# Hybrid streaming encoder layer on one core: a bias table stored from 128 partitions, VectorE in GpSimd's place in the projections, and two steps moved at the start of the windowed attention

## The chip, the cores and the metric

The kernel runs on one core of a Trainium2 chip. The metric is the device time of one execution in microseconds; the time of a kernel is the median of its runs. One execution is also recorded by the hardware profiler, and all durations inside the kernel come from that one.

## The reference

One layer is applied to a prompt of 1024 tokens and to a sample of 64 tokens that continues an older sequence; the width is 1024. Everything is float32.

```
rq, rk, rv, rg, sq, sk, sv, ga, gb = split(rms_norm(x) @ w_in)
A = retention(rope(rq), rope(rk)/16, rv)          # 4 heads of 256, blocks with decay
A = (rms_norm(A) * silu(rg)) @ w_ret_out
s = sq @ sk.T / 8 + bias                          # 16 heads of 64, own chunk of 64 and 128 keys before
B = softmax(s with a learned sink per head) @ sv @ w_swa_out
x += (sigmoid(ga) * A + sigmoid(gb) * B) @ w_mix_out
x += cross_attention(rms_norm(x), memory keys and values)   # 4 heads, 256 memory tokens
x += swiglu(rms_norm(x))
y = rms_norm(x)
```

`bias` is a T5 table of 32 buckets by 16 heads, looked up by the distance of query and key. Retention also returns its last state, the attention its last keys and values, and the memory its keys and values.

## The kernel before

Tokens lie along the free dimension, 1088 of them (1024 and 64), cut into two halves of 544. Each float32 operand of a large product is split into a high part (a cast to fp32r on ScalarE, L124) and a low part (source minus high part on VectorE, L125, in `split`), and a product is three matmuls on TensorE: high by high, high by low, low by high (L223, L224, L226 in `multiply`; L157 to L159 in `mm3`). Large products use Strassen's scheme (`strassen`): seven products of sums of weight blocks. `weight_ops` forms those sums in the raw weight tile, on the engine `sums_by`: VectorE (L191 to L197) until the last query projection, GpSimd (L201 to L207) from there on.

The projections come first (`project_phase`). For each of four retention heads the loop projects keys, queries, and values, the last two lines of each `rotated` step being the sum and difference of the rotary embedding (L649, L650); from the second head on it projects a pair of attention query tiles as well, whose result is multiplied by the token's inverse norm `rstd` (L619 in `project`). Results pass through `stage` tiles to HBM scratch (`d_qkv`, `d_sq`, `d_skv`, `d_gate`). After each head's projections stands `retention(h)`: per block of 256 tokens it loads `ks`, `vf` and `qs` back from `d_qkv`, transposes them on TensorE (`pk`, L768), forms scores (`pss`), the state (`pkv`) and the output (`po`). `ret_out` then normalises the output: ScalarE squares (L890), a row of small VectorE steps (L893, `rsqrt_steps` L320 to L325, L329), ScalarE scales (L896), TensorE turns it back (`pb`, L902). The next head's projections lie between these steps, to keep TensorE occupied.

Between the second and third head stands `bias_table`: a one-hot matmul (L573) looks up the 16 heads' 256 distances, VectorE scales them into `rb` (L574), and one DMA writes `d_rb`, where each head's row of 256 stands 64 times, so that a later load with a stride of 255 reads it shifted per query. The sinks follow (L580 to L585).

`begin_swa` and `swa` are the windowed attention: per half chunk, scores on TensorE (`pss`, L1006, one PSUM tile), add of the bias with minimum and maximum on VectorE (`nm`, L1016), exponentials on ScalarE (L1022, L1024), sum and reciprocal on VectorE (L1025, L1026), scaling on GpSimd (L1028). Pieces of other work fill TensorE between them (`filler`): first the last head of the memory values, `pd` scaled by `mtok` into `swin` (L1202), then the product with `w_ret_out`, whose operands `ret` are loaded and cast by `first_loads` (high parts) and finished by `first_low` (ten low parts, L1155). Those pieces have two PSUM tiles.

The order on each engine is set by a scheduler that models the program's time; `issue_after(x)` holds an instruction behind x in that order. `self.marks` has, for each scores step issued so far, the VectorE instruction that ends its maxima (L1020) and its last exponential; `first_low` is called when two steps have been issued. SyncE's queue (SP) issues most DMAs, in order.

Of the kernel before, what the change touches and what calls it, by code (L numbers as in the profile page):

```python
# [11 lines left out]
F32 = mybir.dt.float32  # L12
F32R = mybir.dt.float32r
AF = mybir.ActivationFunctionType
ALU = mybir.AluOpType
# [4 lines left out]
P = 128  # L20
# [7 lines left out]
BLK = 256  # L28
# [81 lines left out]
class Kernel:  # L110
# [453 lines left out]
    def bias_table(self):  # L564

        nc, io = self.nc, self.io
        t = self.ra.tile([P, BLK + 16], F32, tag="sf", bufs=1, name="table")
        rb = self.ra.tile([P, 2, BLK], F32, tag="o", bufs=1, name="rb")[:16]
        table, onehot = t[:32, BLK:], t[:32, :BLK]
        self.load(table, io["rel_bias"])  # L570
        self.load(onehot, io["c_onehot"])
        pb = self.norm_psum("pb")
        nc.tensor.matmul(pb[:16, :256], table, onehot, start=True, stop=True)  # L573
        nc.vector.tensor_scalar(rb, pb[:16, :256].unsqueeze(1).broadcast_to([16, 2, 256]), 8.0, None, ALU.mult)  # L574
        self.store(self.d_rb.rearrange("h (i c) -> h i c", c=512),
                   rb.rearrange("p a b -> p (a b)").unsqueeze(1).broadcast_to([16, 32, 512]))
        row = self.np.tile([P, 16], F32, tag="row", bufs=1, name="row")[:1]
        self.load(row, io["sinks"])
        ps = self.norm_psum("ps")
        nc.tensor.matmul(ps[:, :16], self.ones[:1, :], row, start=True, stop=True)  # L580
        for e in range(2):
            rows = slice(e * 64, (e + 1) * 64)
            nc.vector.tensor_copy(self.sinks[rows, :], ps[rows, :16].rearrange("p (a b) -> p a b", b=2)[:, :, e])
        self.minus = self.np.tile([P, 16], F32, tag="row", bufs=1, name="minus")[:, :NPAIR]
        nc.vector.tensor_scalar(self.minus, self.sinks, -1.0, None, ALU.mult)  # L585

    def project_phase(self):
        nc, tc, io = self.nc, self.tc, self.io
        with ExitStack() as ctx:
# [11 lines left out]
            half = lambda t: slice(t * HALF, (t + 1) * HALF)  # L601
            flat = lambda o: o.rearrange("p b c -> p (b c)")

            def staged():
                count[0] += 1
                return stage[(count[0] - 1) % len(stage)]

            def taken(ps, sb):
                o = staged()
                if sb is None:  # L610
                    self.last_copy = nc.scalar.copy(o, ps).ins
                else:
                    nc.vector.tensor_tensor(out=o, in0=ps, in1=sb, op=ALU.add)  # L613
                return flat(o)

            def project(w, put, act=None, other=None):
                def emit(i, t, ps, sb):
                    o = taken(ps, sb)
                    (nc.vector if act is not None else nc.gpsimd).tensor_tensor(  # L619
                        out=o, in0=o, in1=self.rstd[:, half(t)], op=ALU.mult)  # L620
                    if act is not None:
                        nc.scalar.activation(o, o, act)
                    if other is not None:
                        r = op.tile([P, HALF], F32, tag="other", bufs=4, name="other")
                        self.load(r, other(i)[:, half(t)])
                        nc.gpsimd.tensor_tensor(out=o, in0=o, in1=r, op=ALU.mult)
                    put(i, t, o)
                cast = self.last_cast
                self.strassen(w, self.ops, emit)
                return cast  # L630

            def rotated(w, h, j, before=None):

                done = {}

                def emit(i, t, ps, sb):
                    done[i, t] = taken(ps, sb)
                    if (1 - i, t) not in done:
                        return
                    a, b = done[0, t], done[1, t]  # L640
                    cos, sin = (rope[:, i, half(t)] for i in range(2))
                    sa, sb = flat(staged()), flat(staged())
                    tt = nc.vector.tensor_tensor
                    tt(out=sa, in0=a, in1=sin, op=ALU.mult)
                    tt(out=sb, in0=b, in1=sin, op=ALU.mult)
                    tt(out=a, in0=a, in1=cos, op=ALU.mult)
                    tt(out=b, in0=b, in1=cos, op=ALU.mult)
                    tt = tt if h < 2 else nc.gpsimd.tensor_tensor
                    tt(out=a, in0=a, in1=sb, op=ALU.subtract)  # L649
                    tt(out=b, in0=b, in1=sa, op=ALU.add)  # L650
                    self.store(self.d_qkv[j, 2 * h, :, half(t)], a)
                    self.store(self.d_qkv[j, 2 * h + 1, :, half(t)], b)
                self.strassen(w, self.ops, emit, before=before)
# [67 lines left out]
            for idx, w, act in ((1, "w_ga", AF.Sigmoid), (0, "w_rg", AF.Silu), (2, "w_gb", AF.Sigmoid)):  # L721
                for m in range(0, KT, 2):
                    if (idx, m) == (1, 6):
# [4 lines left out]
                        op = ctx.enter_context(tc.tile_pool(name="op", bufs=1, reuse_waits="tile"))  # L728
# [399 lines left out]
    def ld(self):  # L1128
        self.lds.append(self.lds.pop(0))
        return self.lds[-1]  # L1130
# [19 lines left out]

    def first_low(self):

        with self.tc.issue_after(self.marks[-1][0]):
            for a, hi, lo in self.first:
                self.nc.vector.tensor_tensor(out=lo, in0=a, in1=hi.bitcast(F32), op=ALU.subtract)  # L1155

# [29 lines left out]
    def filler(self):  # L1186

        nc, tc, io = self.nc, self.tc, self.io
        if True:
            ld, rets = self.ld, self.rets  # L1190
            self.first_low()
            us, h = self.first_units, H - 1
            for t in range(2):
                ps = self.dense_psum()
                for k in range(KT):
                    x = self.ms[k][:, :, t * P:(t + 1) * P]
                    self.mm3(ps[:, :256], x[:, 0], x[:, 1], *us[k // 4][k % 4], k == 0, k == KT - 1)
                    if k == 3:
                        yield
                o = ld()[:, :256]  # L1200
                with tc.high_priority():
                    self.values_out = nc.scalar.mul(o, ps[:, :256], self.mtok[:, t:t + 1]).ins  # L1202
                nc.gpsimd.dma_start(self.d_mv[h, :, t, :], o)
                nc.gpsimd.dma_start(io["o_mv"][t * P:(t + 1) * P, h * 256:(h + 1) * 256], o)
                yield
# [8 lines left out]
            for m, c in order:  # L1214
# [9 lines left out]
                for ps in self.pieces(u, rets, c0, n):  # L1224
                    if step in extra:
                        i, j = extra.pop(step)
# [666 lines left out]
```

## Time and profile before

| | |
|---|---|
| median of 3 runs | 2172.07 us (2171.89 to 2172.37) |
| profiled execution | 2170.14 us, of which the span of its instructions is 2168.3 us |
| mean granted TensorE clock | 0.996 |
| TensorE matmul busy | 2134.6 us (98%) |
| VectorE busy | 1547.7 us (71%) |
| ScalarE busy | 875.0 us (40%) |
| GpSimd busy | 588.8 us (27%) |
| DMA | 290.84 MB, mean 134 GB/s |

In the rows that follow PE is TensorE's matmul, PEld its weight load, DVE VectorE, ACT ScalarE, POOL GpSimd and SP SyncE; a q behind the name is the engine's queue. Times are from the span's start. A row of the groups gives line, engine, operation, tiles, shape and count, then busy time and the mean ns of one, then the idle time in front. A row of the waits gives who waited for whom, then microseconds in total, times, and the longest. A row of the windows gives a stretch, its length, the busy time of PE, PEld, DVE, ACT and POOL with the count of instructions, the granted TensorE clock, the share of the DMA engines and GB/s.

### The profile page before, as it was taken

The page shows a single profiled execution, that of the slowest core. Times are in us where ns is not written, and L with a number is a line of the kernel's source. Part 1 is how long each engine was busy: PE and PEld are TensorE (multiplying, and loading weights), DVE is VectorE, ACT ScalarE, POOL GpSimd, SP SyncE. Part 2 cuts the span into 40 slices and gives each one's busy share as a digit, 9 for nine tenths or more (in the row PEclk, how much of TensorE's full clock was granted, in tenths as well). Part 3 has the DMA queues.
Part 4 walks back from the last instruction along what each step waited for, and adds up shares of the span by engine and source line. Part 5 has one row for each costly group of instructions (what it writes and reads, how often), then busy time and mean ns, then how long its engine had stood idle before and what let it go on. Part 6 is the DMA issues. An engine that isn't in the chain of part 4 may idle for free. (4 is left out here: it accounts for less than half of the span.)

```text
span 2168.3 us, 41740 instructions
## 1 busy us (share of the span) xinstructions
PE 2134.6 (98%) x16371; PEld 2082.8 (96%) x16371; DVE 1547.7 (71%) x2874; ACT 875.0 (40%) x1896; POOL 588.8 (27%) x484
## 2 busy tenths in 40 slices
PE   9999999999999999999999999999999999999997
PEld 9999999999999997889999999999999999999997
DVE  8986978776677558656545565778777777877597
ACT  8333434353434357543233333333322222344243
POOL 0001211233253124540000000015556555523531
PEclk9999999999999999999999999999999999999998
DMA  7334453444345476336442121522342333384333
GB/s 268 118 128 120 135 140 104 138 126 154 120 142 178 154 228 218 119 108 209 133 147 96 40 69 46 161 67 91 126 149 89 105 117 100 117 311 151 112 116 112
DMA packets 169894, 290.84 MB, mean 134 GB/s; under 512 B 39298, under 2 KB 96546, under 8 KB 169698
## 3 DMA queue, kind: packets, MB, share of 16 engines
q1 hardware_dynamic: 161666, 269.00, 38.8%
q0 software_dynamic: 3424, 10.82, 1.4%
q10 hardware_dynamic: 4608, 8.36, 1.0%
q8 instruction: 129, 2.11, 0.4%
q14 instruction: 67, 0.55, 0.1%
HBM read 196.95 MB, written 91.16 MB: 133 GB/s over the span
## 5 line engine op out<-in xcount | busy, mean ns | idle before, releaser
L125 DVE TENSOR_TENSOR wq<-raw,wq 128x512 fp32r<-128x512 f32 (+1 forms) x499 | 435.4, 877 | 131.8 <-ACT wq L124 128.2
L124 ACT CAST wq<-raw 128x512 fp32r<-128x512 f32 (+1 forms) x499 | 301.8, 614 | 539.8 <-PE pq L226 210.5
L224 PE MATMUL pq<-T,wq 128*128 128x272 f32 x1832 | 492.2, 289 | 0.1
L223 PE MATMUL pq<-T,wq 128*128 128x272 f32 x1832 | 490.7, 288 | 1.3 <-DVE stage L613 0.6
L224 PE MATMUL pq<-B,wq 128*128 128x272 f32 x1592 | 427.0, 288 | 0.1
L223 PE MATMUL pq<-B,wq 128*128 128x272 f32 x1592 | 425.7, 288 | 0.0
L226 PE MATMUL pq<-T,wq 128*128 128x272 f32 x1832 | 382.9, 289 | 1.9 <-DVE wq L125 1.9
L223 PEld LDWEIGHTS pq<-T,wq 128*128 128x128 f32 x1832 | 344.4, 188 | 2.1 <-ACT xsq L499 0.8
L224 PEld LDWEIGHTS pq<-T,wq 128*128 128x128 f32 x1832 | 344.2, 188 | 1.2 <-issue 0.8
L226 PE MATMUL pq<-B,wq 128*128 128x272 f32 x1592 | 331.7, 289 | 0.0
L224 PEld LDWEIGHTS pq<-B,wq 128*128 128x128 f32 x1592 | 299.1, 188 | 0.8 <-issue 0.4
L223 PEld LDWEIGHTS pq<-B,wq 128*128 128x128 f32 x1592 | 299.0, 188 | 0.1
L226 PEld LDWEIGHTS pq<-T,wq 128*128 128x128 f32 x1832 | 289.8, 189 | 3.9 <-DVE wq L125 2.4
L201 POOL TENSOR_TENSOR raw<-raw 128x512 f32<-128x512 f32 (+1 forms) x44 | 62.2, 1413 | 802.4 <-DVE rs_r L322 455.6
L226 PEld LDWEIGHTS pq<-B,wq 128*128 128x128 f32 x1592 | 251.7, 189 | 0.9 <-issue 0.7
L274 DVE TENSOR_TENSOR u<-pq,u 128x544 f32<-128x544 f32 x177 | 127.2, 719 | 84.8 <-PE pq L226 84.6
L619 POOL TENSOR_TENSOR stage<-stage,rstd 128x544 f32<-128x544 f32 x20 | 31.6, 1584 | 323.0 <-ACT rstd L514 203.7
L613 DVE TENSOR_TENSOR stage<-pq,u 128x544 f32<-128x544 f32 x112 | 80.3, 718 | 31.6 <-PE pq L226 27.8
L157 PE MATMUL pd<-xc,wq 128*128 128x256 f32 (+1 forms) x256 | 74.5, 291 | 0.0
L1541 POOL TENSOR_TENSOR stage<-stage,rstd_f 128x544 f32<-128x544 f32 x40 | 63.9, 1607 | 39.1 <-ACT stage L1540 39.1
L159 PE MATMUL pd<-xc,wq 128*128 128x256 f32 (+1 forms) x256 | 74.1, 290 | 0.0
L158 PE MATMUL pd<-xc,wq 128*128 128x256 f32 (+1 forms) x256 | 73.7, 288 | 0.0
(391 smaller groups left out, 4587.2 us busy)
## 6 DMA issues: line engine op xcount, KB each, us to landing
hl<-d_op SPq DMA_DIRECT2D x85, 272.0 KB, 5.1
d_qkv<-stage SPq DMA_DIRECT2D x44, 272.0 KB, 2.2
d_op<-stage SPq DMA_DIRECT2D x44, 272.0 KB, 2.5
d_op<-ht SPq DMA_DIRECT2D x44, 272.0 KB, 3.6
raw<-w_gate SPq DMA_DIRECT2D x22, 512.0 KB, 3.5
raw<-w_up SPq DMA_DIRECT2D x22, 512.0 KB, 5.1
raw<-w_down SPq DMA_DIRECT2D x16, 512.0 KB, 4.9
d_gate<-stage ACTq DMA_DIRECT2D x28, 272.0 KB, 2.8
```

Source lines behind the costliest of these rows:

```text
L124: self.last_cast = self.nc.scalar.copy(hi, src).ins
L125: return self.nc.vector.tensor_tensor(out=lo, in0=src, in1=hi.bitcast(F32), op=ALU.subtract).ins
L157: mm(ps, wh, xh, start=start, stop=False)
L158: mm(ps, wh, xl, start=False, stop=False)
L159: self.last_mm = mm(ps, wl, xh, start=False, stop=stop).ins
L201: tt(out=a11, in0=a11, in1=a21, op=sub)
L223: mm(ps[:, c, :HC], w[:, 0, ks], x[:, 0, cs], start=start, stop=False)
L224: mm(ps[:, c, :HC], w[:, 0, ks], x[:, 1, cs], start=False, stop=False)
L226: self.last_mm = mm(ps[:, c, :HC], w[:, 1, ks], x[:, 0, c * HC:(c + 1) * HC], start=False, stop=stop).ins
L274: add = lambda out, a, b: nc.vector.tensor_tensor(out=out, in0=a, in1=b, op=ALU.add)
L613: nc.vector.tensor_tensor(out=o, in0=ps, in1=sb, op=ALU.add)
L1541: nc.gpsimd.tensor_tensor(out=g, in0=g, in1=r[t], op=ALU.mult)
```

## The change

Four edits.

- The bias table is looked up for 128 rows in place of 16: the host repeats each head's column eight times, the matmul has 128 output rows, and the DMA writes each head from eight partitions, four copies of 512 from each, in place of 32 copies from one partition.
- In `project` the multiplication by `rstd` and in `rotated` the last two steps of all heads are VectorE's. Before, GpSimd did 20 of the former and 16 of the latter.
- `first_low` stands behind the first maxima in place of the second.
- The last head's memory values are scaled out of PSUM by VectorE in place of ScalarE.

```diff
 def bias_table(self):
-        t = self.ra.tile([P, BLK + 16], F32, tag="sf", bufs=1, name="table")
-        rb = self.ra.tile([P, 2, BLK], F32, tag="o", bufs=1, name="rb")[:16]
+        t = self.ra.tile([P, BLK + P], F32, tag="sf", bufs=1, name="table")
+        rb = self.ra.tile([P, 2, BLK], F32, tag="o", bufs=1, name="rb")
...
-        nc.tensor.matmul(pb[:16, :256], table, onehot, start=True, stop=True)
-        nc.vector.tensor_scalar(rb, pb[:16, :256].unsqueeze(1).broadcast_to([16, 2, 256]), 8.0, None, ALU.mult)
-        self.store(self.d_rb.rearrange("h (i c) -> h i c", c=512),
-                   rb.rearrange("p a b -> p (a b)").unsqueeze(1).broadcast_to([16, 32, 512]))
+        nc.tensor.matmul(pb[:, :256], table, onehot, start=True, stop=True)
+        nc.vector.tensor_scalar(rb, pb[:, :256].unsqueeze(1).broadcast_to([P, 2, 256]), 8.0, None, ALU.mult)
+        self.store(self.d_rb.rearrange("h (r i c) -> (h r) i c", r=8, i=4),
+                   rb.rearrange("p a b -> p (a b)").unsqueeze(1).broadcast_to([P, 4, 512]))
...
 project.emit
-                    (nc.vector if act is not None else nc.gpsimd).tensor_tensor(
-                        out=o, in0=o, in1=self.rstd[:, half(t)], op=ALU.mult)
+                    nc.vector.tensor_tensor(out=o, in0=o, in1=self.rstd[:, half(t)], op=ALU.mult)
 rotated.emit
-                    tt = tt if h < 2 else nc.gpsimd.tensor_tensor
 first_low
-        with self.tc.issue_after(self.marks[-1][0]):
+        with self.tc.issue_after(self.marks[0][0]):
 filler
-                    self.values_out = nc.scalar.mul(o, ps[:, :256], self.mtok[:, t:t + 1]).ins
+                    self.values_out = nc.vector.tensor_scalar(o, ps[:, :256], self.mtok[:, t:t + 1], None, ALU.mult).ins
 kernel
-    arr["rel_bias"] = a["rel_bias"]
+    arr["rel_bias"] = np.repeat(a["rel_bias"], 8, axis=1)
```

The new text is two lines shorter by L648, so a line there has a number lower by one or two. The scheduler also gives the retention steps of the second and third head other places between the projections; from the last head's first block on TensorE's order is nearly the old one, and from there to the windowed attention it is the same but for the moved steps.

SP's queue before, around the bias table's store (`d_rb`), between the second and third head; `d_sq` are query projections, `vf`, `ks` and `qs` the next block's operands:

```order
L118 DMA table<-rel_bias 32x16
L118 DMA table<-c_onehot 32x256
L121 DMA d_sq<-stage_640 128x32
L121 DMA o_rss<-state 128x2x256
L121 DMA d_ret<-ret_t 128x2x64
L121 DMA d_rb<-rb 512x1x512
...
L118 DMA vf<-d_qkv 128x2x256
...
L118 DMA raw<-w_q 128x1024
L118 DMA ks<-d_qkv 128x2x256
L118 DMA qs<-d_qkv 128x2x256
```

And the same place now:

```order
L118 DMA table<-rel_bias 32x128
L118 DMA table<-c_onehot 32x256
L118 DMA raw<-w_q 128x1024
L121 DMA o_rss<-state 128x2x256
L121 DMA d_ret<-ret_t 128x2x64
L121 DMA d_rb<-rb 512x1x512
L118 DMA vf<-d_qkv 128x2x256
L118 DMA ks<-d_qkv 128x2x256
L118 DMA qs<-d_qkv 128x2x256
```

The stores of `d_sq` that stood between `d_rb` and `ks`, and the weights `w_q`, are ahead of `d_rb` now; the block's operands stand right behind it.

VectorE before, at the start of the windowed attention, from the end of the first maxima (L1016) to the first low parts (L1155):

```order
L1020 TENSOR_TENSOR es<-sinks,nm 128x4
L1025 TENSOR_TENSOR den<-den,es 128x4
L1016 ISA t,nm<-pss,swin_9668,minus 128x64
...
L1026 RECIPROCAL den<-den 128x4
...
L1155 TENSOR_TENSOR wq<-raw,wq 128x512
L1155 TENSOR_TENSOR ret_9680<-swin_9669,ret_9680 128x384
```

And now (L1014 was L1016, L1018 was L1020, L1023 and L1024 were L1025 and L1026, L1153 was L1155, L1200 was L1202, the memory values):

```order
L1018 TENSOR_TENSOR es<-sinks,nm 128x4
L1153 TENSOR_TENSOR wq<-raw,wq 128x512
...
L1153 TENSOR_TENSOR ret_9687<-swin_9672,ret_9687 128x384
L1023 TENSOR_TENSOR den<-den,es 128x4
L1014 ISA t,nm<-pss,swin_9668,minus 128x64
...
L1024 RECIPROCAL den<-den 128x4
L1200 TENSOR_SCALAR swin_9672<-pd,mtok 128x256
L1018 TENSOR_TENSOR es<-sinks,nm 128x4
L1023 TENSOR_TENSOR den<-den,es 128x4
...
L1200 TENSOR_SCALAR swin_9672<-pd,mtok 128x256
```

The ten low parts moved ahead of the first `den` and the second maxima; the two scalings joined VectorE's queue, the first behind the second maxima, the second behind the second `den`. Before, both were ScalarE's, behind the second exponentials.

## The prediction

> **What bounds the kernel now.** I read the head of the page, then TensorE's waits by stage, then the windows and the order of time at the two places that hold most of them.
>
> ```profile
> span 2168.3 us, 41740 instructions
> ...
> PE 2134.6 (98%) x16371; PEld 2082.8 (96%) x16371; DVE 1547.7 (71%) x2874; ACT 875.0 (40%) x1896; POOL 588.8 (27%) x484
> ```
>
> TensorE is the bound: 2134.6 of 2168.3 us. No edit takes work from it, so the change can only bring back idle TensorE time, 33.7 us in all, and of that only what lies where the edits reach. TensorE's waits in the projections of the second to fourth head, 200 to 500 us, are these:
>
> ```profile
> PE pk L768 <- DMA ks<-d_qkv: 2.4, 1, 2.4
> PE pb L902 <- ACT ret_o L896: 2.3, 3, 1.1
> PE pk L768 <- issue: 0.6, 1, 0.6
> PE pss L157 <- DVE rr L322: 0.6, 1, 0.6
> ```
>
> That is 5.9 us, six stops. From 500 to 793 us that view has no row. At the start of the windowed attention, 793 to 850 us, it has these:
>
> ```profile
> PE pss L1006 <- DVE nm L1016: 3.3, 3, 1.4
> PE pd L157 <- ACT swin L1202: 0.9, 1, 0.9
> PE pss L1006 <- DVE stage L613: 0.8, 1, 0.8
> PE pd L157 <- ACT swin L985: 0.7, 1, 0.7
> PE pd L157 <- DVE swin L1231: 0.3, 1, 0.3
> ```
>
> Another 6.0 us. The reader should see that the prize is small: 11.9 us, 0.55% of the time.
>
> **Bias table: the store and who stands behind it.** The windows around it:
>
> ```profile
> 300.00:304.00 4.00, 4.00 (x34) 4.00 (x34) 3.51 (x9) 1.02 (x2) 0.00 (x0) 1.00 0.21 68
> ...
> 308.00:312.00 4.00, 4.00 (x32) 3.83 (x32) 3.16 (x7) 0.62 (x1) 2.54 (x2) 1.00 0.91 101
> ...
> 320.00:324.00 4.00, 4.00 (x35) 4.00 (x34) 2.63 (x5) 1.10 (x2) 0.00 (x0) 1.00 0.94 236
> 324.00:328.00 4.00, 1.59 (x14) 1.41 (x13) 0.13 (x1) 0.79 (x2) 0.00 (x0) 1.00 0.59 207
> ```
>
> And from the DMA issues, with KB and microseconds to landing:
>
> ```profile
> ks<-d_qkv SPq DMA_DIRECT2D x16, 256.0 KB, 2.9
> ...
> d_rb<-rb SPq DMA_DIRECT2D x1, 1024.0 KB, 12.7
> ```
>
> While the store runs, the DMA engines are 91% busy and move 101 GB/s; right after it they move 236. The store takes 12.7 us, everything issued behind it queues, and at 324 to 328 TensorE does 1.59 us in 4: it waits 2.4 us for `ks`. From 128 partitions I price the store at the rate that follows it: 1.05 MB at 236 GB/s is 4.4 us. The ends are 12.7 (nothing gained) and any quicker store, which gains no more than the 2.4.
>
> In the new order `vf`, `ks`, `qs` stand directly behind the store. From the table's matmul to the transposes of that `ks` TensorE has 140 matmuls: at 34 in 4.00 us, 16.5 us. The store is issued some 1.6 us after the table's matmul (an estimate: one VectorE step of 0.7 us and the issue) and lands at 6 to 8. `ks` may be loaded only when the block's scores are done, some 97 matmuls or 11.4 us after the table, and needs 2.9 us: 14.3 or 14.9 with its issue, ahead of 16.5. So the stop goes: 2.4 us, with 1.6 us of slack. With the old 12.7 us the store lands at 14.3, `vf` and `ks` at 1.1 us each behind it, and the stop is some 1 to 2 us. The matmul with 128 output columns in place of 16 and the scaling of 128 rows stream the same 256 and 512 elements: nothing.
>
> **VectorE in GpSimd's place.** The groups of the span, GpSimd's and VectorE's form of the steps, and one like the later scaling of the memory values:
>
> ```profile
> L619 POOL TENSOR_TENSOR stage<-stage,rstd 128x544 f32<-128x544 f32 x20 | 31.6, 1584 | 323.0 <-ACT rstd L514 203.7 <-DVE stage L613 90.9 <-issue 28.4
> ...
> L649 POOL TENSOR_TENSOR stage<-stage,stage 128x544 f32<-128x544 f32 x8 | 13.7, 1707 | 12.2 <-DVE stage L645 5.4 <-DVE rs_v L320 3.6 <-DVE stage L646 1.9
> ...
> L650 POOL TENSOR_TENSOR stage<-stage 128x544 f32<-128x544 f32 x8 | 12.8, 1596 | 83.7 <-DVE stage L644 57.7 <-DVE rs_t L324 22.6 <-DVE stage L647 2.7
> ...
> L650 DVE TENSOR_TENSOR stage<-stage 128x544 f32<-128x544 f32 x8 | 5.7, 716 | 0.0
> ...
> L1312 DVE TENSOR_TENSOR qf<-pd,rstd 128x256 f32<-128x256 f32 x32 | 12.6, 418 | 3.4 <-PE pd L159 3.2
> ```
>
> And the groups of VectorE from 200 to 500 us:
>
> ```profile
> L125 DVE TENSOR_TENSOR wq<-raw,wq 128x512 fp32r<-128x512 f32 x68 | 57.3, 842 | 3.7 <-ACT wq L124 3.4
> ...
> L125 DVE TENSOR_TENSOR ks<-ks 128x512 fp32r<-128x512 f32 x12 | 11.9, 995 | 7.0 <-PE pk L768 5.2 <-issue 1.8
> ...
> L125 DVE TENSOR_TENSOR st<-state,st 128x512 fp32r<-128x512 f32 x9 | 8.4, 936 | 6.3 <-ACT st L124 6.3
> ...
> L193 DVE TENSOR_TENSOR raw<-raw 128x512 f32<-128x512 f32 x8 | 5.5, 687 | 0.1
> ```
>
> GpSimd loses 36 operations, 58.1 us. VectorE gets 36 at 0.716 us: 25.8 us. What it gets back shows in its own means: the same 128x512 form takes 687 ns where GpSimd is quiet (L193), but 842, 995 and 936 in three groups of low parts. That is 68 x 0.155 + 12 x 0.308 + 9 x 0.249 = 16.5 us. One pair in order of time, GpSimd's row and VectorE's, shows why:
>
> ```profile
> 250.69 1.82 POOL L649 TENSOR_TENSOR stage<-stage,stage 128x544 f32<-128x544 f32 x1
> ```
>
> ```profile
> 251.21 1.85 DVE L125 TENSOR_TENSOR st<-state,st 128x512 fp32r<-128x512 f32 x1
> ```
>
> VectorE's step runs 1.85 us beside GpSimd's and ends 0.55 us after it, almost its own length of 0.687: it was held until GpSimd had finished. The Trainium skill, "SBUF — State Buffer", section "Who interferes with whom", says that a VectorE operation with both inputs in SBUF and a GpSimd operation exclude each other for the whole instruction, the second blocked until the first has finished; this pair agrees. By that rule taken whole, up to 58.1 us would come back for 25.8, none of the three kinds of stop below would stay, and the sum would be a microsecond more, 7.6; the sum here goes by the 16.5 of the rows.
>
> So VectorE's load in 300 us rises by about 9 us net, spread thin, and each of these steps is 0.716 us of VectorE's queue where one met by GpSimd cost 1.2 extra at an unlucky moment.
>
> Such moments are what TensorE waits for:
>
> ```profile
> 230.00:265.00 35.00, 32.41 (x260) 31.60 (x260) 32.65 (x62) 14.05 (x33) 7.27 (x5) 1.00 0.43 141
> ...
> 330.00:380.00 50.00, 50.00 (x411) 50.00 (x410) 45.52 (x94) 22.00 (x54) 7.30 (x5) 1.00 0.34 104
> ...
> 410.00:500.00 90.00, 90.00 (x730) 89.31 (x729) 65.48 (x120) 37.27 (x85) 30.03 (x20) 1.00 0.42 119
> ```
>
> In 230 to 265 us VectorE is busy 32.65 of 35, with five GpSimd steps in it, and there TensorE loses 2.6 us: the small normalisation steps stand in VectorE's queue behind held ones, ScalarE's scaling is late, and the turn back (L902) with it. The three rows other than `ks` are 3.5 us. I take 2.5: some of these stops have a cause that stays (the chain of seven small steps in a full queue), and the retention's new places can make small new ones. Bounds: +3.5 and, if new stops outweigh the old, below nothing (the rival). None of the 36 steps adds a wait: the operand was written by VectorE itself or by `rstd` long before; only stores wait for them, sooner. From 410 us on TensorE had no stop (90.00 of 90), and VectorE's 65.48 leave room for the steps of the last head and after.
>
> **The start of the windowed attention.** VectorE in order of time:
>
> ```profile
> 803.58 0.16 DVE L1025 TENSOR_TENSOR den<-den,es 128x4 f32<-128x4 f32 x1 [6.42 <-ACT es L1024]
> ...
> 805.14 0.68 DVE L1155 TENSOR_TENSOR wq<-raw,wq 128x512 fp32r<-128x512 f32 x1
> ...
> 808.22 1.95 DVE L1155 TENSOR_TENSOR ret<-swin,ret 128x384 fp32r<-128x384 f32 x4
> 810.10 0.15 DVE L1025 TENSOR_TENSOR den<-den,es 128x4 f32<-128x4 f32 x1
> ```
>
> TensorE in order of time, and the longest of SP's waits:
>
> ```profile
> 797.01 0.68 PE L1006 MATMUL pss<-swin,swin 64*128 64x64 f32 x8 [1.01 <-DVE nm L1016]
> ...
> 805.92 0.45 PE L157 MATMUL pd<-ret,wq 128*128 128x384 f32 x1 [0.89 <-ACT swin L1202]
> ```
>
> ```profile
> SPq L118 <- DVE ret L1155: 10.9, 2, 10.5
> ```
>
> VectorE stands idle 6.42 us for ScalarE's first exponentials, then does the low parts from 805.14 to 810.10, when TensorE already wants them, and SP's loads of the next operands wait 10.5 us for the first. Now the low parts fill that idle stretch: 5.0 us of work in 6.4, behind casts that ScalarE has done by then or does meanwhile. `den` and the second maxima wait for the same exponentials as before, so nothing is pushed back. The first scaling of memory values, on VectorE, comes about where the first low part stood, at 805.14 or a little before, and takes 0.42 (L1312): TensorE's first `ret` piece, at 805.92 after a wait of 0.89, could start at 805.4 to 805.6. The second scaling stands behind a `den` that waits for ScalarE, but its PSUM tile is wanted a piece of 24 matmuls later, over 2.8 us even at 0.118 each. With the 0.3 of L1231 I take 0.8, between 0 and 1.2.
>
> What follows is 5 us less VectorE backlog, and SP's loads come up to 8 us earlier. Of L1006's 3.3 us, 1.0 (at 797.01) comes before the low parts and stays; 2.3, with the 0.7 of L985, lie behind: 3.0. They come from a full VectorE queue, 8.77 of 10 us as late as 835 to 845 (the first row below), which the same work fills again, so I take less than a third, 0.9, between -1 and 3.0.
>
> ```profile
> 835.00:845.00 10.00, 9.08 (x71) 7.03 (x70) 8.77 (x32) 6.69 (x25) 5.41 (x8) 1.00 0.91 299
> ```
>
> ```profile
> 797.50:801.00 3.50, 3.50 (x20) 3.42 (x19) 0.00 (x0) 3.48 (x8) 1.09 (x3) 0.51 0.36 126
> ```
>
> The sum: 2.4 + 2.5 + 0.8 + 0.9 = 6.6 us. The profiled execution, 2170.14 us (2168.3 of span and 1.8 around it), would become 2163.5; it lies 1.9 below the median of the runs, so I move the median by the same step: 2172.07 - 6.6 = 2165.5.
>
> **Rivals.** (1) VectorE becomes what the projections wait for. In 230 to 265 us, if nothing of the holding came back, five steps of 0.716 would make 36.2 us of work in 35; past that point every normalisation is late, and fifteen turns (five for each of three heads) at the 0.77 us of the three seen cost 11.5 in place of 3.5. With 2.4 from the store and 1.2 at the attention the balance is 4.4 us slower: 2176.5. Against it: the means that fall with GpSimd gone. (2) The gains are taken up again: TensorE stops elsewhere in the rearranged retention, the attention gains nothing, and only the store's 2.4 us remain: 2169.7. For it: 45.52 of 50 in 330 to 380. (3) The store is not quicker, since each of its pieces is still 2 KB: `ks` stays late by about 1.5 of 2.4, 2172.07 - 5.1 = 2167.0. Against it: 236 GB/s behind it. (4) The half clock goes. In 797.5 to 801 (the second row above) the granted clock is 0.51: 3.5 us that would be 1.8 at full clock, so 1.7 us are lost, right behind the stage's first two stops. This mechanism gives 2165.5 - 1.7 = 2163.8 if the stage, shifted by some 5 us, meets the clock's watch differently; since nothing else in the trace shows what decides it, I give it one chance in five. The Trainium skill, "TensorE: Matmul & The Clock Gate", section "What's actually happening", says that the clock is set by free-running windows of 3.4 us, so the same stops can fall within one or across two; the half stretch of 797.5 to 801 agrees in its length, and no row here shows the other case.
>
> **How the numbers follow.** About 0.2%, 4.3 us, is what a measurement of this kernel can tell from no change. The forecast 0.47; (4) 0.20; (3) 0.08; (2) 0.16; (1) 0.09. Faster by more than that are the forecast, (4) and (3): 0.75; within it is (2): 0.16; slower is (1): 0.09. Below, all stops that the edits reach and the half clock: 2.4 + 3.5 + 1.2 + 3.0 + 1.7 = 11.8, so 2160.3. Above, the range takes in (2) and nearly no change, 2171.8, and leaves out (1).
>
> **What would show it.** Right: no wait of `pk` for `ks` and a `d_rb` landing in 4 to 6 us; low parts L125 near 690 ns in 200 to 480 us; L902's waits under 1 us together; L1153 before the first L1023, with VectorE's idle time in front of that under 2 us; `ret`'s first piece less than 0.5 us late. Wrong: a `d_rb` of 10 us or more; VectorE over 95% busy in a window of 230 to 400 us with new waits of L902 or `pss`; the waits of L1006 as long as before.

## The result and the profile after

| | before | after |
|---|---|---|
| median | 2172.01 us (7 runs, 2170.24 to 2172.37) | 2165.01 us (7 runs, 2159.66 to 2168.49) |
| profiled execution, its span | 2170.14, 2168.3 us | 2165.55, 2163.7 us |

The ratio is 0.9965, 95% interval 0.9955 to 0.9976: 7.0 us less, where 6.6 was forecast. Measured again, the changed kernel had 0.9966 (0.9952 to 0.9979). Single runs of one kernel lie several microseconds apart, before too, so the experiments go by the ratio and by the traces. The two profiled executions differ by 4.6 us, and the traces can account for no more than that.

The head of the page of after:

```profile
span 2163.7 us, 41722 instructions
...
PE 2136.0 (99%) x16371; PEld 2084.6 (96%) x16371; DVE 1551.7 (72%) x2912; ACT 874.0 (40%) x1894; POOL 532.4 (25%) x448
```

TensorE's idle time fell from 33.7 to 27.7 us, and its busy time rose by 1.4: the clock was at half rate for longer, see below. TensorE's waits of after, 200 to 500 us, then 500 to 793, then 793 to 850:

```profile
PE po L157 <- DVE ret_t L902: 0.6, 1, 0.6
```

```profile
PE pss L1004 <- DVE nm L1014: 1.0, 1, 1.0
PE pss L1004 <- DVE stage L613: 0.8, 1, 0.8
PE pq L223 <- DVE u L274: 0.3, 1, 0.3
PE pq L223 <- ACT u L277: 0.2, 1, 0.2
```

```profile
PE pss L1004 <- DVE nm L1014: 2.2, 3, 1.4
PE pd L157 <- ACT swin L983: 0.2, 1, 0.2
```

In the projections 5.9 us of stops became 0.6. At the windowed attention, which now begins 5 us sooner so that its first two stops lie ahead of 793, 6.0 became 4.2. The store, among the DMA issues of after:

```profile
d_rb<-rb SPq DMA_DIRECT2D x1, 1024.0 KB, 4.5
```

12.7 us became 4.5. VectorE's share of the projections, 200 to 500 us, before and after (busy PE, PEld, DVE, ACT, POOL), and the low parts there after:

```profile
200.00:500.00 300.00, 294.05 (x2347) 287.06 (x2346) 235.30 (x446) 120.41 (x278) 69.05 (x44) 1.00 0.45 127
```

```profile
200.00:500.00 300.00, 299.44 (x2395) 292.95 (x2394) 241.63 (x493) 124.01 (x284) 11.67 (x8) 1.00 0.44 131
```

```profile
L125 DVE TENSOR_TENSOR wq<-raw,wq 128x512 fp32r<-128x512 f32 x70 | 47.9, 684 | 4.6 <-ACT wq L124 4.4
...
L125 DVE TENSOR_TENSOR ks<-ks 128x512 fp32r<-128x512 f32 x12 | 10.1, 846 | 6.1 <-PE pk L766 6.1
L125 DVE TENSOR_TENSOR qs<-qs 128x512 fp32r<-128x512 f32 x11 | 7.6, 688 | 7.2 <-ACT qs L124 7.1
...
L125 DVE TENSOR_TENSOR st<-state,st 128x512 fp32r<-128x512 f32 x9 | 6.2, 684 | 0.9 <-ACT st L124 0.9
```

GpSimd gave up 57 us, VectorE took on 47 more instructions, and its busy time rose by only 6.3 us. A count over the trace says why: in this stretch 29 of VectorE's steps ran over 150 ns longer than the median of their operation and shape before, 26.5 us longer in all; after, it is 5 steps and 5.2 us. These are called held below.

The start of the windowed attention, VectorE in order of time, and SP's wait for the first low part:

```profile
792.52 0.69 DVE L1153 TENSOR_TENSOR wq<-raw,wq 128x512 fp32r<-128x512 f32 x1
...
795.61 1.95 DVE L1153 TENSOR_TENSOR ret<-swin,ret 128x384 fp32r<-128x384 f32 x4
798.24 0.16 DVE L1023 TENSOR_TENSOR den<-den,es 128x4 f32<-128x4 f32 x1 [0.68 <-ACT es L1022]
...
799.22 0.46 DVE L1200 TENSOR_SCALAR swin<-pd,mtok 128x256 f32<-128x256 f32 x1
```

```profile
SPq L118 <- DVE ret L1153: 2.6, 1, 2.6
```

The low parts fill the idle stretch (6.42 us became 0.68), and SP's 10.5 us became 2.6. And the clock there, in the window of its two half-rate stretches:

```profile
792.31:799.14 6.83, 6.83 (x35) 6.71 (x36) 6.07 (x21) 6.37 (x20) 2.66 (x5) 0.50 0.83 271
```

Before it was one stretch of 3.41 us; in this execution two follow each other.

By the start of the same numbered matmul of TensorE, after leads before by 6.0 us at the 4500th (projections), 4.7 at the 6250th (0.8 lost at 595 to 640 us, 0.5 at 640 to 665), 5.9 at the 6750th (start of the attention, in spite of the second stretch), 4.6 at the 15000th and 3.6 at the 16300th (small waits in the last products), 4.6 at the last.

### The profile page after: what moved, and what is told of

It reads as the page before. It is cut to its first block, busy times and chain, and to the rows that moved or that the text cites. A ratio compares the mean times of both kernels' runs of the same rounds, so it can differ in the third digit from the quotient of the medians.

```text
span 2163.7 us, 41722 instructions
## 1 busy us (share of the span) xinstructions
PE 2136.0 (99%) x16371; PEld 2084.6 (96%) x16371; DVE 1551.7 (72%) x2912; ACT 874.0 (40%) x1894; POOL 532.4 (25%) x448
## 5 line engine op out<-in xcount | busy, mean ns | idle before, releaser
L125 DVE TENSOR_TENSOR wq<-raw,wq 128x512 fp32r<-128x512 f32 (+1 forms) x499 | 426.8, 860 | 139.0 <-ACT wq L124 136.0
L201 POOL TENSOR_TENSOR raw<-raw 128x512 f32<-128x512 f32 (+1 forms) x44 | 64.0, 1454 | 1259.0 <-DVE wq L125 531.4
L157 PE MATMUL pd<-xc,wq 128*128 128x256 f32 (+1 forms) x256 | 74.5, 291 | 0.0
L204 POOL TENSOR_TENSOR raw<-raw 128x512 f32<-128x512 f32 (+1 forms) x44 | 58.9, 1338 | 52.6 <-DVE wq L125 50.1
```

Of the source, the lines that this page charges most:

```text
L125: return self.nc.vector.tensor_tensor(out=lo, in0=src, in1=hi.bitcast(F32), op=ALU.subtract).ins
L157: mm(ps, wh, xh, start=start, stop=False)
L201: tt(out=a11, in0=a11, in1=a21, op=sub)
```

## The experiments

"Lead" is how much earlier than before the 4500th matmul starts, "stops" are TensorE's waits from 200 to 500 us, "store" is the landing of `d_rb`, "clock" counts the half-rate stretches of 3.41 us at the start of the attention, "stage" is the time from the 6250th to the 6750th matmul. Times in us. A ratio is to before on the same chip. Before's median there was 2171.65 beside the four single edits, 2169.50 beside the next four kernels and 2170.59 beside the last three, so medians can be compared only within such a group. In the first 200 us, where no edit acts, the profiles already differ by up to 1.3 us, and the leads contain that.

| kernel | median | ratio to before (95%) | lead | stops | store | clock | stage |
|---|---|---|---|---|---|---|---|
| before | 2172.01 | | | 5.9 | 12.7 | 1 | 75.7 |
| changed | 2165.01 | 0.9965 (0.9955 to 0.9976) | 6.0 | 0.6 | 4.5 | 2 | 74.6 |
| table alone | 2166.03 | 0.9982 (0.9972 to 0.9992) | 2.7 | 2.7 | 4.5 | 2 | 75.0 |
| VectorE alone | 2163.53 | 0.9963 (0.9950 to 0.9975) | 6.6 | 0.0 | 12.3 | 2 | 74.6 |
| low parts alone | 2169.65 | 0.9992 (0.9980 to 1.0004) | -1.4 | 5.5 | 12.8 | 1 | 73.1 |
| memory values alone | 2176.31 | 1.0020 (1.0009 to 1.0030) | 1.5 | 5.3 | 12.7 | 3 | 80.9 |
| changed + small GpSimd steps | 2167.06 | 0.9983 (0.9971 to 0.9995) | 1.9 | 4.1 | 4.9 | 1 | 73.3 |
| VectorE and low parts | 2161.20 | 0.9953 (0.9937 to 0.9969) | 6.3 | 0.0 | 12.2 | 1 | 73.0 |
| changed + piece between | 2163.30 | 0.9963 (0.9948 to 0.9977) | 5.9 | 0.0 | 4.5 | 0 | 71.8 |
| all but VectorE | 2166.28 | 0.9982 (0.9970 to 0.9994) | 2.0 | 3.0 | 4.5 | 2 | 74.5 |
| changed, again | 2162.24 | 0.9966 (0.9952 to 0.9979) | 6.3 | 0.0 | 4.5 | 1 | 74.3 |
| changed + GpSimd's steps again | 2166.68 | 0.9984 (0.9976 to 0.9993) | 0.8 | 3.9 | 4.5 | 1 | 73.1 |
| VectorE, low parts, piece between | 2160.04 | 0.9956 (0.9943 to 0.9968) | 6.8 | 0.2 | 12.3 | 0 | 71.6 |

**Each edit alone.** The diffs are the four parts of the change.

The table:

> The kernel before with the bias table from 128 partitions and nothing else; the order on TensorE, VectorE and SP stays, but for the shapes of the table's own steps. Theory 1 (each edit brings its own term of the prediction): the store lands in 4 to 5 us in place of 12.7, the wait of pk for ks (2.4 us at 327) goes, every other wait of the projections stays at 3.5 us, and the median falls by 2.4 to some 2169.6. Rival (the ks stop went in the changed kernel because the new order brought the loads forward, not because of the quicker store): the store lands sooner but ks still waits behind what is queued between them on SP, the stop stays above 1.5 us, and the median stays within 1 us of 2172.

TensorE's waits of it, 200 to 500 us:

```profile
PE pb L902 <- ACT ret_o L896: 1.8, 2, 1.1
PE pk L768 <- issue: 0.6, 1, 0.6
PE pss L157 <- DVE rr L322: 0.3, 1, 0.3
```

The stop for `ks` is gone with every instruction where it was: between the 2500th and the 2750th matmul it gains 2.6 us, and the other kinds of stop stay. Theory 1 holds: in the old order the slow store was that stop's cause. By the ratio the gain is 3.9 us, 1.7 to 6.1 by its interval; the 2.4 that were expected lie within it.

VectorE's steps:

> The kernel before with VectorE in GpSimd's place in the projections and nothing else; the table still from 16 partitions. Theory 1: low parts of 128x512 fall from 842, 995 and 936 ns to about 690, the three waits of L902 and the one of pss for rr (2.9 us together) go, the store still takes over 10 us to land, and a stop of pk for ks of 1 to 2 us is left; the median falls by 2.5 to 4, to some 2168.8. Rival (the rearranged retention alone brought all of the gain): no stop for ks is left with the slow store either, and the median is within 1.5 us of the changed kernel's without its attention part, about 2166.

SP's queue of it, in order of time, then TensorE at the turn of that `ks`:

```profile
320.78 0.67 SPq L121 DMA_DIRECT2D d_rb<-rb  x1
325.14 0.36 SPq L118 DMA_DIRECT2D vf<-d_qkv  x1
332.17 0.36 SPq L118 DMA_DIRECT2D ks<-d_qkv  x1
```

```profile
337.27 0.60 PE L766 MATMUL pk<-ident,ks 128*128 128x128 f32 x4
```

The slow store lands 12.3 us after its issue, at 333.1, a microsecond after the issue of `ks`; `ks` is turned without a wait. So as to `ks` the rival was right: in the new order nobody waits for it with either store. The edit alone takes away all six stops of the projections: a lead of 6.6 us, and 8.0 by the ratio, as much as the whole change. Whether the other order or the missing GpSimd steps did it, this kernel cannot tell, since it has both.

The low parts:

> The kernel before with the ten low parts behind the first maxima and nothing else. Theory 1: VectorE's idle 6.42 us in front of the first den shrinks to under 2, the waits for nm after 800 us shrink by 1 us or more, and SP's wait of 10.5 us for the first low part falls to some 5; the first piece of ret still waits 0.9 us for ScalarE's scaling of the memory values; the median falls by 1 to 1.5, to some 2170.8. Rival (all of the attention's gain comes from both steps together, and what a single one gives is taken up at the next wait): within 0.5 us of 2172. The granted clock may fall to half for none, one or two stretches of 3.4 us at the start of the stage, which is worth up to 1.7 us either way.

Theory 1 as to the mechanism: its stage takes 73.1 us against 75.7 with the same single half-rate stretch, and the first piece of `ret` no longer waits, although ScalarE still scales the memory values; theory 1 had expected its 0.9 us to stay. The time cannot be told from no change. In its profiled execution the clock was halved a second time, right behind the old stop for `ks`:

```profile
328.02:331.43 3.41, 3.41 (x18) 3.41 (x17) 2.99 (x5) 3.38 (x10) 0.00 (x0) 0.50 0.20 34
```

The memory values:

> The kernel before with the last head's memory values scaled by VectorE in place of ScalarE and nothing else. The low parts stay behind the second maxima, and the scalings now stand behind them in VectorE's queue. Theory 1: without the moved low parts this edit brings nothing or costs: the first scaling comes at about 810 us in place of 805, and the first piece of ret starts at about 810.5 in place of 805.9, so 3 to 4 us are lost there; the median rises to some 2175. Rival (ScalarE's load was what made ret late, and the edit helps by itself): a fall by 0.5 to 1 us, to some 2171.3.

TensorE at the first `ret` piece, and VectorE's scaling in front of it:

```profile
808.79 0.66 PE L157 MATMUL pd<-ret,wq 128*128 128x384 f32 x1 [5.13 <-DVE den L1026]
```

```profile
806.22 1.95 DVE L1155 TENSOR_TENSOR ret<-swin,ret 128x384 fp32r<-128x384 f32 x4
808.10 0.15 DVE L1025 TENSOR_TENSOR den<-den,es 128x4 f32<-128x4 f32 x1
808.17 0.47 DVE L1202 TENSOR_SCALAR swin<-pd,mtok 128x256 f32<-128x256 f32 x1
```

Theory 1 holds: the scaling stands behind the low parts, TensorE waits 5.1 us, and behind that stop the clock is halved for two more stretches. Alone this edit costs 4.3 us.

**Which edits still count together.** VectorE and the low parts, then everything but VectorE:

> Two of the four edits: VectorE in GpSimd's place and the low parts behind the first maxima; the table from 16 partitions, the memory values scaled by ScalarE. Theory after the first four runs (the other two edits bring nothing once these two are in): the store lands in some 12 us and still nobody waits for ks; no wait of ret's first piece for the memory values; the median within 1.5 us of the changed kernel's, 2163.5 to 2166. Rival (the prediction's: each term adds): without the table 1 to 2 us of ks are back, without the values 0.5 us more, so some 2167.5.

> Three of the four edits: the table from 128 partitions, the low parts and the memory values; GpSimd keeps its 36 steps. Theory (table and VectorE's steps each remove the stop for ks, the attention adds its own): ks stop gone, L902 and pss stops of 2 to 3 us as before; the gain is the table's 2.5 plus 0.5 to 2.5 of the attention, so some 2167.5, and the VectorE edit is worth only 3 us on top of these where alone it was worth 6 in the projections. Rival (the edits add without overlap): the median is as far above the changed kernel's as the VectorE edit alone was below before, 6 to 8 us, at 2171 or more.

The two edits have a ratio of 0.9953, at the lower end of the whole change's interval, and no stop in the projections. 2161.20 is 2.3 us below the expected range, but before was as much lower on that chip (2169.50); by the ratios the two edits and the whole change are alike, as the theory said. That table and memory values bring anything beside these two is not shown. Without the VectorE edit three stops of L902, one of `pss` and one of `pk` are left, 3.0 us, and the median is 2166.28, near the theory's 2167.5 and far from the rival's 2171: beside the table's, VectorE's edit is worth some 4 us by the ratios, not 8.

**Held by GpSimd, or another order?** The VectorE edit also moves retention steps. Two kernels give GpSimd work beside VectorE's. The first:

```diff
+            def spare(o):
+                for i in range(0, HALF, HALF // 4):
+                    nc.gpsimd.tensor_tensor(out=self.spare, in0=o[:, i:i + HALF // 4], in1=self.rstd[:, i:i + HALF // 4], op=ALU.mult)
```

> The changed kernel, and beside 32 of VectorE's 36 new steps GpSimd again multiplies the same step's result by the inverse norm, in four pieces of 136 columns into a tile that nothing reads. VectorE's work, the stores and the result stay as changed; the scheduler moves some retention steps (a quarter of the lines by which the change itself differs from before). Theory 1 (GpSimd's steps hold VectorE's, which is what the change took away): low parts of 128x512 in 200 to 500 us go back from 685 ns to over 800, VectorE's busy time there rises by 10 us or more, and at least two stops of L902 or pss, 1.5 us or more together, come back; the median is 2 to 5 us above the changed kernel's. Rival (the other order of the retention's steps is what brought the gain): the means may rise, but TensorE still has under 1 us of stops in 200 to 500, and the median is within 1 us of the changed kernel's.

Its TensorE waits from 200 to 500 us, VectorE's longest there, and the low parts:

```profile
PE pb L911 <- ACT ret_o L905: 3.9, 2, 2.2
```

```profile
DVE stage L613 <- POOL spare L618: 10.4, 4, 4.2
```

```profile
L125 DVE TENSOR_TENSOR wq<-raw,wq 128x512 fp32r<-128x512 f32 x69 | 49.3, 714 | 1.2 <-ACT wq L124 1.0
```

Stops and time came back as theory 1 said, but not by its way: the means rose to 714 ns, not over 800, and the two stops stand behind waits of VectorE, 4.2 and 2.7 us, for a `stage` tile that GpSimd still read in four pieces. Short GpSimd steps hold VectorE little each: 42 steps by 13.5 us in all, where before had 29 by 26.5. So the second kernel has whole steps:

```diff
+                    if act is None:
+                        nc.gpsimd.tensor_tensor(out=o, in0=o, in1=self.ones[:, :1].broadcast_to([P, HALF]), op=ALU.mult)
```

(and the same for the two results of the rotation in the last two heads.)

> The changed kernel, and GpSimd multiplies each of the 36 results once more by one, in place and in full length, before it is stored: VectorE's steps as changed, GpSimd's steps as before, the values unchanged. Theory 1 (GpSimd's long steps hold VectorE's, and the stops come from that): low parts of 128x512 in 200 to 500 us take 830 to 1000 ns again in place of 685, VectorE is busy over 255 of 300 us there in place of 241, and TensorE has 2 us or more of stops of L902 or pss; the median is 2 to 5 us above the changed kernel's. Rival (order): the means rise but the stops stay under 1 us together and the median within 1.5 us of the changed kernel's.

Its TensorE waits, GpSimd's group and the low parts, and VectorE's window:

```profile
PE pq L223 <- DVE stage L613: 2.2, 2, 1.1
PE pss L157 <- DVE kt L803: 0.9, 2, 0.6
PE pss L157 <- ACT qs L124: 0.8, 1, 0.8
```

```profile
L621 POOL TENSOR_TENSOR stage<-stage,ones 128x544 f32<-128x544 f32 x20 | 25.8, 1295 | 323.3 <-DVE stage L619 312.5 <-DVE rs_t L323 6.9 <-DVE rr L329 3.2
```

```profile
L125 DVE TENSOR_TENSOR wq<-raw,wq 128x512 fp32r<-128x512 f32 x69 | 48.3, 700 | 5.8 <-ACT wq L124 5.7
```

```profile
200.00:500.00 300.00, 296.07 (x2360) 289.50 (x2360) 249.67 (x481) 121.06 (x275) 64.79 (x44) 1.00 0.42 126
```

No run of it (2164.38 at the lowest) was below the slowest of the changed kernel beside it (2164.18). VectorE is busy 8 us longer with twelve steps fewer in the window, 27 of them held by 18.1 us in all, and stops of 3.9 us are back, other ones than before. The held steps are mostly the rotation's, those by `rstd` and some low parts of `ss`, `ks` and `qs`; the weights' low parts that theory 1 named stay at 700 ns, and the 255 us expected of VectorE were 249.7.

The holding itself follows GpSimd's steps in every profile: 28 to 30 held steps and 24.8 to 27.1 us in the five with GpSimd's steps as before, 4 or 5 steps and 4.3 to 5.2 us in the six without them. The stops follow the holding less closely. Of the five of this kernel only the first, 0.3 us at 234.8, stands right behind held steps. The other four, 3.6 us, stand behind a late load or in a row of VectorE steps of which none is held, two of them (1.05 and 0.60) after this wait for the store of a `stage` tile:

```profile
DVE stage L613 <- DMA d_qkv<-stage: 2.6, 1, 2.6
```

GpSimd's added step also stands between a result and its store, and SP's queue waits for it:

```profile
SPq L121 <- POOL stage L653: 45.8, 5, 19.6
```

That is a second way to the same stops, which neither kernel separates from the holding. So VectorE's time comes back with GpSimd's steps, and TensorE's stops and the median do too, but by which way is open. Nor is it shown that GpSimd's steps are the whole of the gain: by position, 1242 of TensorE's matmuls stand elsewhere in this kernel than in the changed one (1086 in the first kernel), nearly as many as the change itself moves (1443), and a kernel with GpSimd's steps in exactly the new order was not tried.

**The clock.** One piece of the memory values between the first two scores:

```diff
-                yield []
-                yield [pieces] * 6
+                yield [pieces]
+                yield [pieces] * 5
```

> The changed kernel with one piece of the memory values (12 matmuls, 1.4 us) between the first and the second scores of the windowed attention in place of behind both. Theory (the two stops of about 1 us, 2.2 us together within 3.4, are what sets the granted clock to half there): the second stop goes, 1.2 us; the half clock goes or falls to one stretch; from the stage's first scores to 860 us TensorE needs 1.2 to 4 us less, and the median falls to 2161.5 to 2164. Rival (VectorE's chain of maxima, exponentials and low parts sets the stage's pace): the second maxima come 1 us later, the stop moves to the scores or the ret pieces behind them, and the median is within 1 us of the changed kernel's.

Beside it the changed kernel as it is, once more, and the same piece with the two edits that count (VectorE and the low parts) on the kernel before:

> The changed kernel once more, beside the two kernels that follow and on the same chip. All theories expect its time as measured first, 2165 within 3 us; of interest are the stretches of half clock at the start of the windowed attention (none, one or two of 3.41 us) and what the stage from its first scores takes with them: 74.6 us for the first part of 500 matmuls with two, and by the runs with the low parts moved some 73 with one.

> VectorE in GpSimd's place, the low parts behind the first maxima, and one piece of the memory values between the first two scores; table and memory values as before. Theory: it has what the earlier runs showed to bring time and nothing else; no stop in 200 to 500 us, one stop of 1 us in place of two at the first scores, no half clock there; 2160 to 2162.5, 2 to 4 us below the changed kernel on the same chip. Rival (the run that showed no half clock was luck, and the stage is set by VectorE): within 1.5 us of the changed kernel.

TensorE of the last of these in order of time, and the clock there:

```profile
788.66 0.66 PE L1004 MATMUL pss<-swin,swin 64*128 64x64 f32 x8 [0.82 <-DVE stage L613]
789.25 0.39 PE L157 MATMUL pd<-wq,ms 128*128 128x256 f32 x1
```

```profile
788.00:800.00 12.00, 10.61 (x83) 10.14 (x84) 10.37 (x35) 11.42 (x34) 5.49 (x10) 1.00 0.83 261
```

Both kernels with the piece run the stage at full clock; all eleven profiles without it have one to three half-rate stretches there. With the low parts moved the stage takes 74.5 to 74.6 us with two stretches, 73.0 to 74.3 with one, 71.6 to 71.8 with none. The price of one stretch does not come out of these numbers, since the kernels with none also have the second stop filled, and since `ret`'s first piece then waits, 0.89 us in the first and 0.73 in the second, as the rival said of the stops. With the low parts in their old place one stretch (75.7) was no better than two (75.0, 74.6): with one, TensorE waited 0.9 and 0.3 us for pieces of `ret`, with two it did not. So the piece shortens the stage by 1.4 to 2.8 us, within the theory's 1.2 to 4; in the time no gain is shown, with a ratio of 0.9963 beside the changed kernel's 0.9965 and 0.9966. The last kernel has the lowest median, 2160.04 against 2162.24 for the changed kernel on the same chip; by their ratios it and the kernel of two edits are alike, and both intervals overlap the changed kernel's.

The changed kernel's other profile shows what the fourth edit does when the clock is halved only once. TensorE and VectorE in order of time:

```profile
799.93 0.42 PE L157 MATMUL pd<-ret,wq 128*128 128x384 f32 x1 [1.09 <-ACT t L1020]
```

```profile
798.33 0.16 DVE L1023 TENSOR_TENSOR den<-den,es 128x4 f32<-128x4 f32 x1 [0.68 <-ACT es L1022]
...
799.32 0.46 DVE L1200 TENSOR_SCALAR swin<-pd,mtok 128x256 f32<-128x256 f32 x1
```

The `ret` piece needs the PSUM tile that L1200 frees at 799.78, and L1200 stands behind a `den` that waits for ScalarE's exponentials. The view names ScalarE's exponential as the releaser; by time it is L1200. With ScalarE scaling, the kernel of two edits has no such wait, and its stage is 1.3 us shorter, with one stretch as well; with the piece, ScalarE's scaling has one of 0.73 us too. The two kernels with GpSimd's work added have VectorE's scaling, one stretch and no such wait (73.3 and 73.1), so the edit's cost comes and goes; no profile shows a gain from it.

## Why the prediction was right

The time was right, 2165.5 against 2165.01, and so was the bound: the gain is idle TensorE time in two places. That the two numbers lie half a microsecond apart is luck: the ratio's interval allows a gain of 5.2 to 9.8 us, and the terms came out differently. In the profile of after the projections gave 6.0 us where the sum had 4.9, the start of the attention 1.1 where it had 1.7.

- **The store, 2.4 us.** Right that it lands in 4 to 6 us (4.5), that the stop goes, and that 128 partitions are the reason it is quicker: both stores are 512 pieces of 2 KB, and in the table's kernel the order is the old one. That 4.4 us was worked out is in part luck: the pieces themselves ran at 364 GB/s, not 236, for 2.9 us, and the rest of the 4.5 lies before and behind them. The Trainium skill, "SBUF — State Buffer", section "Door 1: The DMA port swizzle (why `[64,N]` ≈ `[32,N]`)", says that a DMA's rate depends on how many of the 16 SBUF ports its partitions reach; 1 MB in 12.7 and in 4.5 us, issue and landing included, agree with it. Wrong was the step "with the old 12.7 us ... the stop is some 1 to 2 us". By the prediction's own figures, 14.3 and twice 1.1 against 16.5, there would have been none, and the kernel with VectorE's edit alone has the old store and no stop. `ks` was turned 18.1 us after the table's matmul (319.2 to 337.3), not 16.5, and its load waited for the scores, not the store. So VectorE's edit takes the same stop away as the table's; the sum holds because it counted that stop once.
- **VectorE in GpSimd's place, 2.5 us.** Too small. The three other rows' 3.5 us went to 0.6 or nothing in every kernel with this edit and without GpSimd's steps, and the `ks` stop with them: a lead of 5.9 to 6.8 us. The load rose by 6.3 us net, where "about 9" was worked out. That GpSimd holds VectorE's steps is shown. That TensorE's stops come from it, "the small normalisation steps stand in VectorE's queue behind held ones", holds for half of them before: the stops at 256.6 and 261.2 us, 1.7 together, stand behind held steps, but those at 240.2 and 405.1, 1.2 together, behind VectorE steps of which none is held, and for the 0.6 of `pk` the profile shows no cause. A held step ahead of 261.2, and what VectorE's rows ahead of the two others begin with:

```profile
258.24 1.61 DVE L125 TENSOR_TENSOR wq<-raw,wq 128x512 fp32r<-128x512 f32 x1
```

```profile
233.17 0.73 DVE L613 TENSOR_TENSOR stage<-pq,u 128x544 f32<-128x544 f32 x1 [1.47 <-DMA d_qkv<-stage]
```

```profile
400.39 0.69 DVE L125 TENSOR_TENSOR qs<-qs 128x512 fp32r<-128x512 f32 x1 [2.79 <-ACT qs L124]
```

So something beside the holding has a part in this term, the other order or the stores that stood behind GpSimd; how large it is, is open. The Trainium skill, same page, section "Who interferes with whom", has the lock last for one instruction. The quarter-length steps agree: a held step was held by 0.32 us on average, where before it was 0.91, and the only three held by more than 0.6 us stood beside whole GpSimd steps that are left there.
- **The start of the attention, 0.8.** The low parts alone take 2.6 us off the stage with one half-rate stretch; with two, the edits bring 0.4 at most (75.0 and 74.6 without them, 74.6 with). Wrong was that the scaling by VectorE brings part of it: "`ret`'s first piece less than 0.5 us late" held in the profile of after, and not in the second, where it waits 1.09.
- **The later attention, 0.9.** The wait of L985 went from 0.7 to 0.2. The waits for `nm` hardly changed, 3.3 to 3.2, which the prediction named as a sign against it: that part of the term failed, and behind the low parts the trace shows 0.6 us in place of 0.9 (2.3 became 2.2, and 0.7 became 0.2).
- **Rival (4), the half clock.** At one in five it was over-rated as a by-product: no profile that keeps the first stops is without it, and in the profile of after it lasted twice as long. Nor is it worth its full 1.7 us there: in the changed kernel's other profile, with one stretch, the stage is 0.3 us shorter and `ret` waits instead. It went in both kernels that fill the second stop.
- **Rivals (1) and (3)** fell with VectorE's 241.6 of 300 us and the store's 4.5. **Rival (2)** fell: most of the gain is not the store's.
- Not foreseen were small losses elsewhere in the profile of after: 1.3 us at 595 to 665 us and 2.2 between the 14000th and the 16300th matmul. Both are absent from its second profile, so they come and go between executions of the same kernel; what causes them is not shown.

## What to carry to other kernels

When several edits aim at the same stops, test each alone: here one of them already had the whole gain, one was superfluous beside it and one cost time by itself. Where a second engine's steps hold those of the engine in front of the bound one, read the worth of moving them in the first engine's busy time (6.3 us more here) and not in the sum of durations (25.8); but look at each stop's own queue, since half of the stops here stood behind no held step. Two stops of 1 us close together can cost more than 2 us, since the clock falls behind them; a piece of independent work between them brought the clock and 1.4 to 2.8 us of the stage back, though no time that could be told from the changed kernel's.

## What the runs showed of the hardware

- The TensorE clock comes in stretches that are multiples of 3.413 us (half rate for 3.413 or 6.827 here, full rate for 785.065 before it in the profile of after). Two stops of together 1.8 us (0.82 and 1.01), with eight small matmuls behind each, sufficed to halve it in nine profiles, one of 1.80 between two such groups in two more; the 0.82 alone, in the two kernels with the piece, did not. Whether one or two stretches follow changes from execution to execution of one kernel, and goes by where the second scores fall: in the seven profiles with one stretch (of memory values alone the first is meant) they begin 0.2 to 1.5 us before it, in the four with two from 0.02 us before to 0.14 behind its start. The stop for `ks` fits too, when the stretches are counted back in steps of 3.413 us: the one of 2.1 us that was followed by half rate (low parts alone) lies within one step, those of 2.4 and 2.5 that were not (before, memory values alone) are cut in two, 1.6 and 0.8, 1.8 and 0.7. The Trainium skill, "TensorE: Matmul & The Clock Gate", section "What's actually happening", has a free-running window of 3413 ns, which agrees, and the slow state after an idle window; here the window was not idle, so by the measurement less than an idle window is enough.
- A slower TensorE can cost nothing: with the low parts in their old place, behind the second maxima, the stage was no slower with two half-rate stretches (75.0 and 74.6 us) than with one (75.7).
- In two profiles (table alone, memory values alone) the 128x384 matmuls between the 7000th and the 9000th came every 178.2 ns on average, in all others every 175.4: 2.7 us, at a granted clock of 1.00 and with no wait in the trace. Its cause is open.
